# Gates of both token blocks of a recurrence unit computed together, recurrences one step later

## The chip, the cores and the metric

The kernel runs on one core of one Trainium2 chip. A core has five engines, each with its own in-order queue: TensorE (PE in the profile, with its weight loads shown as PEld), VectorE (DVE), ScalarE (ACT), GpSimd (POOL) and SyncE (SP, which issues the DMAs). The metric is the device time of one execution in microseconds; lower is better.

## The reference

One decoder layer on 2048 tokens of width 1024, in float32. Two token mixers work side by side on one input projection: four heads of a gated linear recurrence with a 128x128 state (HGRN2), and a gated real recurrence of width 512 behind a causal convolution (RG-LRU). Then come an output projection, a SwiGLU feed-forward of width 2816 and a final norm.

```python
xn = rms_norm(h, mix_norm_w)
q, f_logit, i_v, g, lru_x, lru_gate = split(xn @ w_in)
# HGRN2, per head, chunks of 32 tokens
f = lb + (1 - lb) * sigmoid(f_logit);  k = 1 - f;  b = cumsum(log(f))
scores = tril((silu(q) * exp(b)) @ (k * exp(-b)).T)
o = scores @ v + (silu(q) * exp(b)) @ state
state = exp(b_last) * state + (k * exp(b_last - b)).T @ v
# RG-LRU, width 512
xc = causal_conv4(lru_x) + conv_b
r = sigmoid(blockdiag(wa) @ xc + ba);  ig = sigmoid(blockdiag(wx) @ xc + bx)
a = exp(-8 * r * softplus(-a_param))
h_t = a * h_{t-1} + sqrt(1 - a*a) * (ig * xc)
y = h * gelu(lru_gate)
h = h + concat(rms(o) * silu(g), y) @ w_out
h = h + (silu(gate) * up) @ w_down;  out = rms_norm(h)
```

## The kernel before

The sequence is worked in two halves of 1024 tokens, each of two blocks of 512 (`c` = 0, 1). For each half the mixer runs first: values `v` (tiles `pv`), then eight steps `s` = 0 to 7, then the output gate (`pg`), the transposes `tp_o` and the output projection (`po` with a half number, `poh` in the profile). After both mixers come the feed-forward stages of both halves (`quad_*`, `pda`, `pdb`). Every 128x512 product is three matmuls per 128 rows of contraction (a high part times high and low part, and low times high), so a projection of one block (`feat_mm`, tiles `pa` and `pb`) is 24 matmuls.

Even steps work one HGRN2 head, odd steps one RG-LRU unit (128 of the 512 channels). A tile's name carries its step and its block: `lg_4_0` belongs to step 4, block 0. For each step and block the code computes `pa`, calls `run_pending`, computes `pb`, and then the first part of the step:

- HGRN2, `hg_pre`: ACT takes two sigmoids (`sq`, `sf`), a logarithm (`lg`, L257) and four exponentials (`eb` L262, `nx` L279 and L278, `lg` L280); DVE takes a running sum (`b`) and some fifteen products, the last of the line that PE needs being `lg` at L315. Its later parts wait in the list `pend`: `hg_mid` (PE transposes `lg` into `pk`, L329; products `pc`; DVE copies `pk` to `kut`; PE forms `pu` from it) and `hg_post` (PE forms `po`).
- RG-LRU, `lru_pre`: convolution on DVE, the GeLU branch `gl` on ACT, and a split of `xc` into `xh` and `xl`. Its later part is one function, `lru_post`: six matmuls into `pr` and `pi`, two sigmoids (`r`, `ig`), a tanh (`t`), an exponential (over `r`), DVE products, a square root (over `t`), a scan and the product `y`.

`run_pending` calls the next part of everything in `pend`, so `lru_post` of block 0 is written into block 1 of the same step, and that of block 1 into block 0 of the next step, which is an HGRN2 step.

[...]

The order in which the instructions of one engine stand is not the order of the code: a scheduler orders them when the program is built, by a model of its own, and on the chip every engine then takes its queue strictly in that order. The pools matter to it: tag `pg` has 16 pages of 128x512, tag `late` has 5, and PSUM has 4 banks under the tag `mm` (for `pa`, `pb`, `pg`) and 4 under `aux` (for `pr`, `pi`, `pk`, `pc`, `pu`, `po`, `tp_o`).

Of the kernel before, what the change touches and what calls it, by code (L numbers as in the profile page):

```python
# [35 lines left out]
def hybrid_layer(ctx: ExitStack, tc: tile.TileContext, x, x_t, norm_w, cols, w_in, gate_w, w_out, w_gu, w_down, out):  # L36
# [10 lines left out]
    def page(nm, dt=F32):  # L47
        return sb.tile([P, CW], dt, tag="pg", name=nm, bufs=16)
# [5 lines left out]
    def block(nm, dt=F32R):  # L54
        return sb.tile([P, 4, CW], dt, tag="bt", name=nm, bufs=14)
# [7 lines left out]
    def late(nm):  # L63
        return sb.tile([P, CW], F32, tag="late", name=nm, bufs=5)
# [4 lines left out]
    def aux(nm):  # L69
        return psp.tile([P, CW], F32, tag="aux", name=nm)  # L70
# [142 lines left out]
    def act_tile(nm):  # L213
        return [[block(f"{nm}_{s}{n}") for n in range(2)] for s in range(2)]

    def part(xt, s, k, ts=slice(0, CW)):
        return xt[s][k // 4][:, k % 4, ts]
# [7 lines left out]
    def transpose_in(dst, tt, n, src, nm, scale=None):  # L225
        split([dst[s][n][:, :, tt * P : (tt + 1) * P] for s in range(2)], transposed(tt, n, src, nm), scale)

    def feat_mm(w, xt, nm):
        ps = bank(nm)
        whi, wlo = w  # L230
        for k in range(KT):
            hi, lo = part(xt, 0, k), part(xt, 1, k)
            ks = slice(k * P, (k + 1) * P)
            nc.tensor.matmul(ps, lhsT=whi[:, ks], rhs=hi, start=(k == 0), stop=False)  # L234
            nc.tensor.matmul(ps, lhsT=wlo[:, ks], rhs=hi, start=False, stop=False)  # L235
            nc.tensor.matmul(ps, lhsT=whi[:, ks], rhs=lo, start=False, stop=(k == KT - 1))  # L236
        return ps

    def tok_mm(w4, xt, tt, nm):
        ps = bank(nm)  # L240
        tsl = slice(tt * P, (tt + 1) * P)
        for k in range(KT):
            whi, wlo = w4[k // 2]
            ks = slice((k % 2) * CW, (k % 2 + 1) * CW)
            hi, lo = part(xt, 0, k, tsl), part(xt, 1, k, tsl)
            nc.tensor.matmul(ps, lhsT=hi, rhs=whi[:, ks], start=(k == 0), stop=False)  # L246
            nc.tensor.matmul(ps, lhsT=hi, rhs=wlo[:, ks], start=False, stop=False)  # L247
            nc.tensor.matmul(ps, lhsT=lo, rhs=whi[:, ks], start=False, stop=(k == KT - 1))  # L248
        return ps
# [115 lines left out]
    def hg_post(h, st, vt, nm):  # L365
        hs = slice(h * P, (h + 1) * P)
        QI, S, sc = st["QI"], st["S"], st["sc"]
        po = aux("po" + nm)
        for n in range(TPC):
            ns = slice(n * P, (n + 1) * P)  # L370
            nc.tensor.matmul(po[:, ns], lhsT=QI[:, ns], rhs=S[n], start=True, stop=False)
            nc.tensor.matmul(po[:, ns], lhsT=sc[:, n, :], rhs=vt[:, n, hs], start=False, stop=True)
        ss = small.tile([P, TPC], F32, tag="oss", name="oss" + nm)
        jk = late("ojk" + nm)
        for n in range(TPC):
            ns = slice(n * P, (n + 1) * P)
            nc.scalar.activation(out=jk[:, ns], in_=po[:, ns], func=AF.Square, scale=float(P) ** -0.5, accum_out=ss[:, n : n + 1])
        v.tensor_scalar(out=ss, in0=ss, scalar1=EPS, scalar2=None, op0=ALU.add)
        nc.gpsimd.tensor_tensor(out=ss, in0=ss, in1=mhalf, op=ALU.pow)
        v.tensor_tensor(  # L380
            out=vt[:, :, hs], in0=po.rearrange("p (n e) -> p n e", e=P), in1=ss.unsqueeze(2).broadcast_to([P, TPC, P]), op=ALU.mult
        )


    def lru_pre(u, psx, psg, nm):
        xp = sb.tile([P, CW + 4], F32, tag="pg", name="xp" + nm, bufs=16)
        v.tensor_copy(out=xp[:, 0:3], in_=hist[:, u, :])
        nc.scalar.copy(out=xp[:, 3 : 3 + CW], in_=psx)
        nc.gpsimd.tensor_copy(out=hist[:, u, :], in_=xp[:, CW : CW + 3])
        gl = page("gl" + nm)  # L390
        nc.scalar.activation(out=gl, in_=psg, func=AF.Gelu_apprx_tanh)
        xc = page("xc" + nm)

        def cw(k):
            return par[:, C_CONVW + k * 4 + u : C_CONVW + k * 4 + u + 1]

        v.tensor_scalar(
            out=xc, in0=xp[:, 0:CW], scalar1=cw(0), scalar2=par[:, C_CONVB + u : C_CONVB + u + 1], op0=ALU.mult, op1=ALU.add
        )
        for k in range(1, 4):  # L400
            v.scalar_tensor_tensor(out=xc, in0=xp[:, k : k + CW], scalar=cw(k), in1=xc, op0=ALU.mult, op1=ALU.add)
        xh, xl = page("xh" + nm, dt=F32R), page("xl" + nm, dt=F32R)
        split((xh, xl), xc)
        return gl, xc, xh, xl


    def lru_post(u, gl, xc, xh, xl, y, nm):
        pr, pi = aux("pr" + nm), aux("pi" + nm)
        for m, pg in enumerate((pr, pi)):
            gs = slice((m * NU + u) * P, (m * NU + u + 1) * P)  # L410
            nc.tensor.matmul(pg, lhsT=gwh[:, gs], rhs=xh, start=True, stop=False)
            nc.tensor.matmul(pg, lhsT=gwl[:, gs], rhs=xh, start=False, stop=False)
            nc.tensor.matmul(pg, lhsT=gwh[:, gs], rhs=xl, start=False, stop=True)
        r, ig, t = late("r" + nm), late("ig" + nm), late("t" + nm)
        us = slice(u, u + 1)
        nc.scalar.activation(out=r, in_=pr, func=AF.Sigmoid, bias=par[:, C_BA + u : C_BA + u + 1])
        nc.scalar.activation(out=ig, in_=pi, func=AF.Sigmoid, bias=par[:, C_BX + u : C_BX + u + 1])

        nc.scalar.activation(out=t, in_=r, func=AF.Tanh, scale=msp[:, us])
        nc.scalar.activation(out=r, in_=r, func=AF.Exp, scale=nmsp[:, us])  # L420
        v.tensor_tensor(out=ig, in0=ig, in1=xc, op=ALU.mult)
        v.tensor_tensor(out=xc, in0=r, in1=r, op=ALU.mult)
        v.scalar_tensor_tensor(out=t, in0=xc, scalar=1.0, in1=t, op0=ALU.add, op1=ALU.mult)
        nc.scalar.activation(out=t, in_=t, func=AF.Sqrt)
        v.tensor_tensor(out=ig, in0=ig, in1=t, op=ALU.mult)
        v.tensor_tensor_scan(out=t, data0=r, data1=ig, initial=hst[:, us], op0=ALU.mult, op1=ALU.add)
        nc.gpsimd.tensor_copy(out=hst[:, us], in_=t[:, CW - 1 : CW])
        v.tensor_tensor(out=y[:, u, :], in0=t, in1=gl, op=ALU.mult)
# [505 lines left out]
    for half in range(2):  # L934
# [26 lines left out]
                    later.pop(0)()  # L961
        ys = [block(f"y{half}_{c}", F32) for c in range(NC)]

        pend = []

        def run_pending():
            for p in pend:
                p.pop(0)()
            pend[:] = [p for p in pend if p]

        for s in range(8):
            i = s // 2
            ws.ahead(2)
            wa, wb = ws.take(2)
            ws.ahead(2)
            for c in range(NC):
                nm = f"{half}_{s}_{c}"
                pa = feat_mm(wa, xt[c], "pa" + nm)
                run_pending()
                pb = feat_mm(wb, xt[c], "pb" + nm)  # L980
                if s % 2 == 0:
                    st = hg_pre(i, pa, pb, nm)
                    nxt = [
                        lambda i=i, st=st, c=c, nm=nm: hg_mid(i, c, st, vts[c], nm),
                        lambda i=i, st=st, c=c, nm=nm: hg_post(i, st, vts[c], nm),
                    ]
                else:
                    r = lru_pre(i, pa, pb, nm)
                    nxt = [lambda i=i, r=r, c=c, nm=nm: lru_post(i, *r, ys[c], nm)]
                pend.append(nxt)  # L990
        wg = ws.take(4)
        mixes = []
        for c in range(NC):
            for tt in range(TPC):
                ps = tok_mm(wg, xt[c], tt, f"pg{half}_{c}_{tt}")
                run_pending()
                sg = page(f"sg{half}_{c}_{tt}")
                nc.scalar.activation(out=sg, in_=ps, func=AF.Silu)
                v.tensor_tensor(out=vts[c][:, tt, :], in0=vts[c][:, tt, :], in1=sg, op=ALU.mult)
            mx = act_tile(f"mx{half}_{c}")  # L1000
            for tt in range(TPC):
                transpose_in(mx, tt, 0, vts[c][:, tt, :], f"o{half}_{c}_{tt}", par[:, C_HN : C_HN + 1])
            for u in range(NU):
                split([part(mx, s, 4 + u) for s in range(2)], ys[c][:, u, :])
            mixes.append(mx)
# [30 lines left out]
        for c in range(NC):  # L1036
            todo = len(steps[c])
            for n in range(2):
                wo = ws.take(4)
                for tt in range(TPC):  # L1040
                    g = c * TPC + tt
                    nm = f"h{half}_{g}_{n}"
# [14 lines left out]
                    i = n * TPC + tt + 1  # L1057
# [108 lines left out]
```

## Time and profile before

| | before |
|---|---|
| median of three runs | 2135.84 us (2135.84 to 2138.68) |
| profiled execution | 2136.71 us, span of its instructions 2135.0 us |
| TensorE busy | 2104.3 us, 99% of the span |
| VectorE busy | 1493.7 us, 70% |
| ScalarE busy | 1010.3 us, 47% |
| mean granted TensorE clock | 0.995 |
| first mixer, about 60 to 340 us; second, about 470 to 740 us | steps 0 to 7, then `pg` |

TensorE is busy nearly all the time, so what matters is where it isn't, and where its granted clock (1.00 is full speed) drops. The timeline gives each instruction's start and length in microseconds, and in brackets how long its engine was idle before it and who ended the wait. A matmul's length is longer than its distance to the next one, since matmuls overlap; distances between starts are what counts.

### The profile page before, as it was taken

Reading aid. Unit: us, or ns where it says so; the run is one execution under the profiler, and the core shown is the slowest. Engines: PE = TensorE matmul, PEld = TensorE weight load, DVE = VectorE, ACT = ScalarE, POOL = GpSimd, SP = SyncE. Lnnn points to the kernel's source line nnn. Section 1 sums busy time; section 2 is a strip of 40 time slices with the busy share of each in tenths; the row PEclk is TensorE's granted clock in tenths of the full one; section 3 lists DMA queues with packets and bytes.
Section 4 is the critical chain, followed back from the end, with each engine's and each line's share of the span. In section 5 each row is a group of like instructions: output and inputs, shape, how many; then the busy total and the mean of one; then the engine's idle time right before and its main releaser. Section 6 shows DMA issues by size and latency. Waiting matters only on the chain.

```text
span 2135.0 us, 26155 instructions
## 1 busy us (share of the span) xinstructions
PE 2104.3 (99%) x9704; PEld 1737.9 (81%) x9704; DVE 1493.7 (70%) x2415; ACT 1010.3 (47%) x1647; POOL 84.7 (4%) x130
## 2 busy tenths in 40 slices
PE   8999999999999999999999999999999999999998
PEld 6887888888877888788888888888788888888887
DVE  6577664645777566877667669878867667669787
ACT  5577764536777644533333334335333333334333
POOL 2000000100000000000000000000000000000000
PEclk9999999999999999999999999999999999999999
DMA  6111105851101058433223266345423223257424
GB/s 221 56 40 40 40 20 167 288 160 57 40 30 40 20 191 263 146 102 124 98 89 114 89 218 231 114 138 186 144 94 113 98 87 127 94 202 253 157 88 143
DMA packets 138420, 262.84 MB, mean 123 GB/s; under 512 B 11186, under 2 KB 27570, under 8 KB 138292
## 3 DMA queue, kind: packets, MB, share of 16 engines
q1 hardware_dynamic: 138292, 261.17, 36.6%
q8 instruction: 76, 1.25, 0.2%
q14 instruction: 52, 0.43, 0.1%
HBM read 197.95 MB, written 63.18 MB: 122 GB/s over the span
## 4 chain that ended last, share of the span: by engine, by line
PE 87%; ACT 6%; DVE 5%; DMA 1%; issue 1%; SPq 0%; POOL 0%; DVEq 0%; POOLq 0%; ACTq 0%
PE quad_e L614 11%; PE quad_g L614 11%; PE quad_a L614 11%; PE pda L882 10%; PE pdb L882 7%; PE quad_f L614 6%; PE poh L247 3%; PE poh L248 3%; PE poh L246 3%; PE pb L234 2%; PE pb L236 2%; PE pb L235 2%; PE pa L234 1%; PE pa L235 1%; PE pg L248 1%; PE pg L246 1%
## 5 line engine op out<-in xcount | busy, mean ns | idle before, releaser
L614 PE MATMUL quad_e<-act_e,wgu_e 128*128 128x512 f32 x528 | 129.6, 395 | 1.9 <-ACT wgu_e L207 1.9
L614 PE MATMUL quad_f<-act_f,wgu_f 128*128 128x512 f32 x528 | 127.9, 390 | 2.2 <-ACT wgu_f L207 1.5
L614 PE MATMUL quad_a<-act_a,wgu_a 128*128 128x512 f32 x528 | 127.5, 389 | 0.0
L614 PE MATMUL quad_g<-act_g,wgu_g 128*128 128x512 f32 x528 | 127.5, 390 | 0.0
L614 PE MATMUL quad_a<-act_b,wgu_b 128*128 128x512 f32 x528 | 127.3, 389 | 0.0
L614 PE MATMUL quad_g<-act_d,wgu_d 128*128 128x512 f32 x528 | 127.0, 389 | 0.1
L614 PE MATMUL quad_e<-act_c,wgu_c 128*128 128x512 f32 x528 | 126.9, 389 | 0.0
L614 PEld LDWEIGHTS quad_e<-act_e,wgu_e 128*128 128x128 f32 x528 | 100.4, 191 | 23.6 <-ACT wgu_e L207 2.4
L614 PEld LDWEIGHTS quad_f<-act_f,wgu_f 128*128 128x128 f32 x528 | 99.2, 188 | 23.9 <-ACT wgu_f L207 1.8
L498 DVE TENSOR_TENSOR u<-u,quad_g 128x512 f32<-128x512 f32 x88 | 60.5, 687 | 81.9 <-PE quad_g L614 81.9
L614 PEld LDWEIGHTS quad_g<-act_d,wgu_d 128*128 128x128 f32 x528 | 99.0, 188 | 21.0 <-DVE u L498 0.5
L614 PEld LDWEIGHTS quad_g<-act_g,wgu_g 128*128 128x128 f32 x528 | 99.1, 188 | 20.8 <-DVE wgu_g L208 0.3
L614 PEld LDWEIGHTS quad_a<-act_b,wgu_b 128*128 128x128 f32 x528 | 99.2, 188 | 20.6
L614 PEld LDWEIGHTS quad_e<-act_c,wgu_c 128*128 128x128 f32 x528 | 99.1, 188 | 20.6
L614 PEld LDWEIGHTS quad_a<-act_a,wgu_a 128*128 128x128 f32 x528 | 99.0, 188 | 20.5
L234 PE MATMUL pa<-xn,whi_in 128*128 128x512 f32 x256 | 102.0, 398 | 0.0
L234 PE MATMUL pb<-xn,whi_in 128*128 128x512 f32 x256 | 101.5, 397 | 0.0
L235 PE MATMUL pb<-xn,wlo_in 128*128 128x512 f32 x256 | 101.3, 396 | 0.0
L236 PE MATMUL pb<-xn,whi_in 128*128 128x512 f32 x256 | 101.2, 395 | 0.0
L235 PE MATMUL pa<-xn,wlo_in 128*128 128x512 f32 x256 | 100.8, 394 | 0.0
L236 PE MATMUL pa<-xn,whi_in 128*128 128x512 f32 x256 | 100.8, 394 | 0.0
L247 PE MATMUL poh<-wlo_o,mx 128*128 128x512 f32 x256 | 99.8, 393 | 0.6 <-DVE wlo_o L164 0.6
(331 smaller groups left out, 4944.6 us busy)
## 6 DMA issues: line engine op xcount, KB each, us to landing
raw<-in_w_gu SPq DMA_DIRECT2D x88, 512.0 KB, 3.8
raw_in<-in_w_in SPq DMA_DIRECT2D x48, 512.0 KB, 3.5
ao_p<-as SPq DMA_DIRECT2D x76, 256.0 KB, 2.6
raw_o<-in_w_out SPq DMA_DIRECT2D x32, 512.0 KB, 4.5
x<-in_x SPq DMA_DIRECT2D x32, 256.0 KB, 6.0
xrh<-in_x SPq DMA_DIRECT2D x32, 256.0 KB, 3.9
h<-h SPq DMA_DIRECT2D x32, 256.0 KB, 3.7
hn<-hths SPq DMA_DIRECT2D x32, 256.0 KB, 3.4
```

Of the source, the lines that this page charges most:

```text
L234: nc.tensor.matmul(ps, lhsT=whi[:, ks], rhs=hi, start=(k == 0), stop=False)
L235: nc.tensor.matmul(ps, lhsT=wlo[:, ks], rhs=hi, start=False, stop=False)
L236: nc.tensor.matmul(ps, lhsT=whi[:, ks], rhs=lo, start=False, stop=(k == KT - 1))
L246: nc.tensor.matmul(ps, lhsT=hi, rhs=whi[:, ks], start=(k == 0), stop=False)
L247: nc.tensor.matmul(ps, lhsT=hi, rhs=wlo[:, ks], start=False, stop=False)
L248: nc.tensor.matmul(ps, lhsT=lo, rhs=whi[:, ks], start=False, stop=(k == KT - 1))
L498: (e or v).tensor_tensor(out=out, in0=a, in1=b, op=op)
L614: nc.tensor.matmul(ps, lhsT=w[:, s, ks], rhs=x, start=first and k + n == 0, stop=k == 3 and n == 2, skip_group_check=not first)
L882: nc.tensor.matmul(ps, lhsT=x, rhs=y, start=first and q + n == 0, stop=q == gr.n - 1 and n == 2, skip_group_check=not first)
```

## The change

`lru_post` is cut into three: `lru_gates` (the six matmuls, both sigmoids, the tanh), `lru_exp` (the exponential) and `lru_end` (the rest). The gates of block 0 are held back by one place in `pend`, so that the gates of both blocks of a unit are written at the same place, in block 0 of the following step, behind its `pa`. The exponentials of both follow at the end of that block, and `lru_end` of both in its block 1 (after step 7: in the first tiles of `pg`). `r` and `ig` move from the pool of 5 to the pool of 16 pages. The arithmetic is the same.

```diff
-    def lru_post(u, gl, xc, xh, xl, y, nm):
+    def lru_gates(u, gl, xc, xh, xl, nm):
...
-        r, ig, t = late("r" + nm), late("ig" + nm), late("t" + nm)
+        r, ig, t = page("r" + nm), page("ig" + nm), late("t" + nm)
...
         nc.scalar.activation(out=t, in_=r, func=AF.Tanh, scale=msp[:, us])
+        return r, ig, t
+
+    def lru_exp(u, r, ig, t, xc):
+        us = slice(u, u + 1)
         nc.scalar.activation(out=r, in_=r, func=AF.Exp, scale=nmsp[:, us])
+
+    def lru_end(u, r, ig, t, gl, xc, y):
...
+        def gates(i, r, c, nm):
+            gated.append((i, c, lru_gates(i, *r, nm), r[0], r[1]))
+
+        def run_exp():
+            for i, c, (r, ig, t), gl, xc in gated:
+                lru_exp(i, r, ig, t, xc)
+            done = gated[:]
+            gated.clear()
+            if done:
+                pend.append([lambda: [lru_end(i, r, ig, t, gl, xc, ys[c]) for i, c, (r, ig, t), gl, xc in done]])
...
-                    nxt = [lambda i=i, r=r, c=c, nm=nm: lru_post(i, *r, ys[c], nm)]
+                    nxt = [lambda i=i, r=r, c=c, nm=nm: gates(i, r, c, nm)]
+                    if c == 0:
+                        nxt.insert(0, lambda: None)
                 pend.append(nxt)
+                run_exp()
...
                 run_pending()
+                run_exp()
```

What the scheduler made of it differs from the written order, and it is the same in both halves. The built program has 119 table loads on ACT instead of 115. Three places show what moved.

The first place is ACT's queue between the gates of step 3 and the logarithm of step 4. Before, it begins behind all of `r_3_0` (which stands ahead of `xh_3_1`):

```order
L424 ACTIVATE t_3_0_1553<-t_3_0_1553 128x512
L416 ACT_TABLE_LOAD
L416 ACTIVATE r_3_1_1651<-pr_3_1_1643,par 128x512
L417 ACTIVATE ig_3_1_1652<-pi_3_1_1644,par 128x512
L419 ACTIVATE t_3_1_1653<-r_3_1_1651,tinies 128x512
L420 ACT_TABLE_LOAD
L420 ACTIVATE r_3_1_1651<-r_3_1_1651,tinies 128x512
L255 ACT_TABLE_LOAD
L255 ACTIVATE sf_4_0_1692<-pb_4_0_1666 128x512
L257 ACT_TABLE_LOAD
L257 ACTIVATE lg_4_0_1693<-sf_4_0_1692,tinies 128x512
```

Now, on the same engine, from the exponential of block 0 on (its sigmoids and tanh stand just ahead):

```order
L425 ACTIVATE r_3_0_1628<-r_3_0_1628,tinies 128x512
L417 ACT_TABLE_LOAD
L417 ACTIVATE r_3_1_1642<-pr_3_1_1634,par 128x512
L420 ACTIVATE t_3_1_1644<-r_3_1_1642,tinies 128x512
L432 ACT_TABLE_LOAD
L432 ACTIVATE t_3_0_1630<-t_3_0_1630 128x512
L418 ACT_TABLE_LOAD
L418 ACTIVATE ig_3_1_1643<-pi_3_1_1635,par 128x512
L254 ACTIVATE sq_4_0_1673<-pa_4_0_1595 128x512
L425 ACT_TABLE_LOAD
L425 ACTIVATE r_3_1_1642<-r_3_1_1642,tinies 128x512
L255 ACT_TABLE_LOAD
```

The work of both blocks now stands between `xh_3_1` and the logarithm of step 4, and block 0's exponential is still taken ahead of block 1's sigmoid, with a load on each side.

The second place is PE's queue around the transposes `pk_4_0`, the first thing that PE needs of head step 4's chain. Before:

```order
L236 MATMUL pa_5_0_1866<-xn_0_11_165,whi_in_14_1608 128x512
L329 MATMUL pk_4_0_1756<-ident,lg_4_0_1693 128x128 x4
L337 MATMUL pc_4_0_1763<-W_4_0_1716,nx_4_0_1702 64x128
L337 MATMUL pc_4_0_1763<-eb_4_0_1701,nx_4_0_1702 64x64
L234 MATMUL pa_5_0_1866<-xn_0_01_163,whi_in_14_1608 128x512
```

Now:

```order
L236 MATMUL pb_5_0_1942<-xn_0_10_164,whi_in_15_1591 128x512
L329 MATMUL pk_4_0_1740<-ident,lg_4_0_1675 128x128 x4
L337 MATMUL pc_4_0_1747<-W_4_0_1698,nx_4_0_1684 64x128
L337 MATMUL pc_4_0_1747<-eb_4_0_1683,nx_4_0_1684 64x64
L234 MATMUL pb_5_0_1942<-xn_0_00_162,whi_in_15_1591 128x512
```

Before, `pk_4_0` stood behind 21 of the 24 matmuls of `pa_5_0`; now it stands behind all 24 and 6 of `pb_5_0`, 9 matmuls later. In the same way `pk_2_0` moves from 8 to 7 matmuls of `pb_3_0`, and `pk_6_0` from 18 of `pa_7_0` to 24 and 7 of `pb_7_0`. The gates of both blocks of a unit stand behind `pa` of the next step (in step 4, `pr_3_0` right behind the last matmul of `pa_4_0`) and in its `pb`; after step 7 they stand behind `pg` tile 0 and in tile 1.

The third place is ACT's queue in the `pg` tiles behind step 7. Before:

```order
L998 ACTIVATE sg_0_1_2658<-pg_0_1_2633 128x512
L416 ACT_TABLE_LOAD
L416 ACTIVATE r_7_1_2615<-pr_7_1_2607,par 128x512
L417 ACTIVATE ig_7_1_2616<-pi_7_1_2608,par 128x512
L419 ACTIVATE t_7_1_2617<-r_7_1_2615,tinies 128x512
L420 ACT_TABLE_LOAD
L420 ACTIVATE r_7_1_2615<-r_7_1_2615,tinies 128x512
L424 ACT_TABLE_LOAD
L424 ACTIVATE t_7_1_2617<-t_7_1_2617 128x512
L998 ACT_TABLE_LOAD
L998 ACTIVATE sg_0_2_2686<-pg_0_2_2661 128x512
```

Now:

```order
L418 ACTIVATE ig_7_1_2607<-pi_7_1_2599,par 128x512
L1021 ACT_TABLE_LOAD
L1021 ACTIVATE sg_0_0_2614<-pg_0_0_2559 128x512
L425 ACT_TABLE_LOAD
L425 ACTIVATE r_7_1_2606<-r_7_1_2606,tinies 128x512
L1021 ACT_TABLE_LOAD
L1021 ACTIVATE sg_0_1_2658<-pg_0_1_2617 128x512
L432 ACT_TABLE_LOAD
L432 ACTIVATE t_7_1_2608<-t_7_1_2608 128x512
L1021 ACT_TABLE_LOAD
L1021 ACTIVATE sg_0_2_2686<-pg_0_2_2661 128x512
```

`sg` is the SiLU of an output gate tile; DVE multiplies it into `v` (L999, now L1022), and PE transposes that into `tp_o`. Before, only block 1's part of unit 7 stood ahead of `sg_0_2`; now both blocks' parts do, and the SiLUs stand between exponential and square root. The queues of SP and POOL, and so the DMA issues, stand in the same order as before.

More of the change, by code (lines that the diff above doesn't have):

```diff
@@ L419, in lru_post @@
         nc.scalar.activation(out=t, in_=r, func=AF.Tanh, scale=msp[:, us])
+        return r, ig, t
+    def lru_exp(u, r, ig, t, xc):
+        us = slice(u, u + 1)
         nc.scalar.activation(out=r, in_=r, func=AF.Exp, scale=nmsp[:, us])
+    def lru_end(u, r, ig, t, gl, xc, y):
+        us = slice(u, u + 1)
         v.tensor_tensor(out=ig, in0=ig, in1=xc, op=ALU.mult)
@@ L962, in hybrid_layer @@
         ys = [block(f"y{half}_{c}", F32) for c in range(NC)]
-        pend = []
+        pend, gated = [], []
+        def gates(i, r, c, nm):
[7 more added lines that the diff above has]
+                pend.append([lambda: [lru_end(i, r, ig, t, gl, xc, ys[c]) for i, c, (r, ig, t), gl, xc in done]])
         def run_pending():
```

## The prediction

> **What bounds the kernel now.** I read the page's busy shares first, then TensorE's list of waits, then its windows around the waits, then ACT's and DVE's timeline in them.
>
> ```profile
> span 2135.0 us, 26155 instructions
> PE 2104.3 (99%) x9704; PEld 1737.9 (81%) x9704; DVE 1493.7 (70%) x2415; ACT 1010.3 (47%) x1647; POOL 84.7 (4%) x130
> ...
> PE pk L329 <- DVE lg L315: 6.4, 3, 2.9
> ...
> PE pu L354 <- DVE kut L331: 3.8, 2, 1.9
> ```
>
> PE is idle for 30.7 us of 2135.0 in all. No matmul is added or removed, so the change can act only through these idle times, through new ones, and through PE's clock. In the mixers the waits are those of `pk` for the end of the head's chain on DVE (`lg`, L315), and of `pu` for the copy behind it. The windows (columns: length, PE busy, clock, then DMA) show where, two per half:
>
> ```profile
> 200.00:212.00 12.00, 9.13 (x50) 0.86 0.28 89
> 264.00:273.00 9.00, 6.46 (x35) 1.00 0.00 1
> 612.00:628.00 16.00, 13.09 (x64) 0.89 0.20 67
> 680.00:692.00 12.00, 10.12 (x47) 0.86 0.09 32
> ```
>
> PE is idle in them for 2.87, 2.54, 2.91 and 1.88 us, 10.2 in all: head step 4 and head step 6 of each half. In three of them the clock fell too: 12 x 0.14, 16 x 0.11 and 12 x 0.14 us are each about 1.7 us of PE time lost on top. In the second it stayed at 1.00. So a wait of some 3 us costs about 4.6. [...]
>
> **The mechanism.** Before `pk`, ACT must finish the head's chain, and the RG-LRU work of the step before stands in ACT's queue among it. ACT's timeline gives each step's price as the distance to the next start:
>
> ```profile
> 174.73 0.69 ACT L416 ACTIVATE r<-pr,par 128x512 f32<-128x512 f32 x1
> 175.32 0.68 ACT L417 ACTIVATE ig<-pi,par 128x512 f32<-128x512 f32 x1
> 175.88 0.72 ACT L419 ACTIVATE t<-r,tinies 128x512 f32<-128x512 f32 x1
> ...
> 178.43 0.72 ACT L420 ACTIVATE r<-r,tinies 128x512 f32<-128x512 f32 x1
> 179.18 1.28 ACT L254 ACT_TABLE_LOAD   x1
> 180.47 0.60 ACT L254 ACTIVATE sq<-pa 128x512 f32<-128x512 f32 x1
> ...
> 182.38 0.63 ACT L424 ACTIVATE t<-t 128x512 f32<-128x512 f32 x1
> ...
> 191.46 0.82 ACT L257 ACTIVATE lg<-sf,tinies 128x512 f32<-128x512 f32 x1
> ...
> 195.53 0.63 ACT L262 ACTIVATE eb<-b 128x512 f32<-128x512 f32 x1
> ...
> 196.38 0.40 ACT L278 ACTIVATE nx<-lg 128x256 f32<-128x256 f32 x1
> 196.81 0.63 ACT L280 ACTIVATE lg<-lg 128x512 f32<-128x512 f32 x1
> 197.46 1.28 ACT L254 ACT_TABLE_LOAD   x1
> ...
> 199.25 1.04 ACT L163 CAST whi_in<-raw_in 128x1024 fp32r<-128x1024 f32 x1
> ...
> 266.00 0.63 ACT L262 ACTIVATE eb<-b 128x512 f32<-128x512 f32 x1 [0.45 <-DVE b L259]
> ```
>
> So: `r` 0.59, `ig` 0.56, `t` 0.74, exponential of `r` 0.75, a load 1.29, `sq` (also `sf`, `sg`) 0.61, square root 0.65, `lg` 0.83, `eb` with the first `nx` 0.85, second `nx` 0.43, last exponential 0.65, cast 1.05, and 0.45 for `b` where no other work covers it.
>
> ```profile
> L424 ACT ACT_TABLE_LOAD x16 | 20.5, 1283 | 0.3
> ```
>
> Sixteen loads have 0.3 us of idling ahead of them in all, and the activation behind one starts with its end (179.18 + 1.28 to 180.47). [...]
>
> DVE's steps behind it (a step is 0.08 shorter than its length, as 198.75 to 199.89 shows):
>
> ```profile
> 195.46 1.28 DVE L426 TENSOR_TENSOR_SCAN t<-r,hst,ig 128x512 f32<-128x512 f32 x1
> ...
> 198.75 1.22 DVE L164 TENSOR_TENSOR wlo_in<-raw_in,whi_in 128x1024 fp32r<-128x1024 f32 x1
> 199.89 0.42 DVE L314 TENSOR_TENSOR lg<-sf,lg 128x256 f32<-128x256 f32 x1
> ...
> 200.63 0.68 DVE L256 TENSOR_TENSOR sq<-sq,pa 128x512 f32<-128x512 f32 x1
> ...
> 201.50 0.29 DVE L318 TENSOR_TENSOR lg<-lg,G 128x128 f32<-128x128 f32 x1
> ...
> 202.45 0.42 DVE L315 TENSOR_TENSOR lg<-nx,G 128x256 f32<-128x256 f32 x1
> ```
>
> **When PE starts the chains, and when it needs them.** In the changed order the gates of block 0 stand right behind `pa` of the head step, so the new chain starts when `pr` ends. At these rows of before, PE has done the same work as after the new `pi` (the last: `pg`, plus its 24 matmuls):
>
> ```profile
> 121.05 0.39 PE L234 MATMUL pb<-xn,whi_in 128*128 128x512 f32 x1
> ...
> 177.47 0.39 PE L234 MATMUL pb<-xn,whi_in 128*128 128x512 f32 x1
> ...
> 237.71 0.39 PE L234 MATMUL pb<-xn,whi_in 128*128 128x512 f32 x1
> 243.15 0.39 PE L234 MATMUL pa<-xn,whi_in 128*128 128x512 f32 x1
> ...
> 290.48 0.39 PE L246 MATMUL pg<-whi_in,xn 128*128 128x512 f32 x1
> ```
>
> 24 matmuls take 5.44 us (237.71 to 243.15), 0.227 each. The last matmul of `pr` starts four steps before these rows and lasts 0.39: `pr` is there at 120.54 (step 2), 176.96 (step 4), 237.20 (step 6) and 290.48 + 5.44 - 0.51 = 295.41 (`pg`). PE reaches the places that wait at:
>
> ```profile
> 146.04 0.60 PE L329 MATMUL pk<-ident,lg 128*128 128x128 f32 x4
> ...
> 199.76 0.39 PE L236 MATMUL pa<-xn,whi_in 128*128 128x512 f32 x1
> 203.02 0.63 PE L329 MATMUL pk<-ident,lg 128*128 128x128 f32 x4 [2.87 <-DVE lg L315]
> ...
> 259.53 0.60 PE L329 MATMUL pk<-ident,lg 128*128 128x128 f32 x4
> ...
> 313.66 1.47 PE L222 MATMUL tp_o<-ident,v 128*128 128x128 f32 x12
> ```
>
> With the new places of `pk` (1 matmul earlier, 9 and 13 later): 145.8, 200.15 + 2.04 = 202.2, 259.53 + 2.95 = 262.5; the third group of `tp_o`, 8 of 12 transposes in, at 314.5. Times are in the frame of before; a wait at one place moves all that is behind it alike.
>
> **The change part by part.** Splitting the function, the list `gated` and the pages cost no instruction. Six matmuls per block move behind the next `pa`: PE does the same work. The four extra loads are 5 us of ACT, inside the chains. SP and POOL keep their order, so no DMA moves. With `r` and `ig` in pages, 8 RG-LRU pages and 8 of a head fill the 16; I find no wait in the queues that this adds on another engine, and bound it by 0 and the longest new wait. Odd steps lose block 0's gates on ACT and DVE; nobody on PE waits there, so that gains nothing. What counts are four chains per half:
>
> - Step 2. ACT: `r`, `ig`, `t`, exponential, square root, then `r`, `ig`, `sq`, `t`, `sf`, exponential, `lg`, 0.45 for `b`, `eb` and `nx`, square root, `nx`, last exponential: 11.0 us, and 8 loads, 10.3. From 120.54 that ends at 141.9. Then a load and `sq` of block 1 (1.9), for which DVE stands: `sq` 0.60, scan 1.20, two half-size steps 0.68, a tiny one 0.07, a quarter 0.20, `y` 0.60, `wlo` 1.14, L315 0.42, together 4.9. `pk` can go at 148.7 against 145.8: 2.9 us, where before has none.
> - Step 4. The first load waits for `pr`. 17 ACT steps with the cast, 11.6, and 10 loads, 12.9: from 176.96 to 201.5; load and `sq` 1.9; DVE 3.4 (no scan, no `y`). 206.8 against 202.2: 4.6.
> - Step 6. The same without the cast, with `b`: 11.0 and 11 loads 14.2: 237.20 to 262.4; 1.9; DVE 4.9. 269.2 against 262.5: 6.7. The later wait for `kut` goes, since its copy then has 22 matmuls of time.
> - `pg`. To the end of block 1's square root 7.8 of steps and 9 loads, 11.6: 295.41 to 314.8; DVE product 0.61, scan 1.20, `y` 0.60, product with `sg` 0.69, and the `tp_o` group can go at about 318.0 against 314.5: 3.5, where before has none.
>
> That is 17.7 us per half, 35.4 in all, against 10.2: plus 25.2. Each of the eight waits is as long as those that let the clock fall, against three before. Five falls at 1.7 are 8.5. A fall's price lies between 0 (the window at 264) and, behind a longer wait, an estimated twice 1.7; I take 1.7, the value of three of four windows. Sum 33.7. The profiled execution took 2136.7, 0.9 above the median of the runs: 2170.4, so I say 2170.
>
> **Rivals.**
> - Faster. The later place of `pk` decides: if the new chain in step 4 ended no later than the old one (L315 near 202.9), the wait there would be 0.7 instead of 2.9 and the clock would hold: 3.9 us less per half, with the waits of step 6 gone too (2.5 and 1.9 + 1.7), 13.9 in all: 2123. Against it: ACT would have to be done near 197.5 in step 4, 4 us before the row sum, and ACT has no gap to give. 3 in 100.
> - No change beyond 0.2% (about what a measurement of this kernel can tell from none, 4.3 us): the waits only move, 2136. It needs chains about 3 us shorter throughout. 4 in 100.
> - Half of it: the chains are 1.5 us shorter at each place and steps 2 and `pg` keep their clock: 12 and 6.8 less, about 2151. 8 in 100 for 2141 to 2151.
> - More: the five new falls twice as dear, and each of the eight chains 1 us longer from waits for pages: 8.5 + 8 more, 2187 and up. 5 in 100.
> - A load holds ACT for twice its row: 82 x 1.28 = 105 more, about 2275. The rows speak against it. 1 in 100.
>
> **How the numbers follow.** The forecast holds 79 in 100 between 2151 and 2187: its ends are 1.5 us off each chain with two falls less, and the dearer falls with 1 us on each. Faster by over 0.2% 0.03, within 0.04, slower 0.93.
>
> **What would show it.** Right: PE's waits for `lg` L315 at six places, about 14 us per half, the longest in step 6; two waits of `tp_o`, 3 to 4 us; the clock under 0.9 around most; ACT with 119 loads. Wrong: `tp_o` and step 2 without waits (the chain's price is too high), or a clock of 1.00 behind them. What I may have missed is a wait inside ACT's chain for DVE or a page, which would make every term longer.

## The result, and the profile after

The changed kernel takes 2176.1 us (median of 4 runs, 2175.3 to 2177.4), against 2137.3 us for the kernel before in the same session: a ratio of 1.0179 (95% interval 1.0167 to 1.0191), 38.8 us more. The forecast was 2170 with a range of 2151 to 2187.

The busy shares of the changed kernel, to be held against those of before:

```profile
span 2174.0 us, 26170 instructions
PE 2114.8 (97%) x9704; PEld 1746.3 (80%) x9704; DVE 1495.9 (69%) x2415; ACT 1016.6 (47%) x1651; POOL 83.7 (4%) x130
```

The span grew by 39.0 us. PE's matmuls are as many as before, and so the whole difference splits in two: PE is idle for 2174.0 - 2114.8 = 59.2 us instead of 30.7 (28.5 more), and busy for 2114.8 instead of 2104.3 (10.5 more, for the same work: mostly a lower clock, as the windows further down show). PE's list of waits (total, times, longest) says where the idle time is:

```profile
PE pk L329 <- DVE lg L315: 30.6, 6, 7.1
PE tp_o L222 <- DVE v L1022: 8.1, 2, 4.0
```

These eight waits make 38.7 us. Before, the waits of the mixers made 11.1: 6.4 of `pk`, 3.8 of `pu` for `kut` and 0.9 of `po` for `sct`. The last two are gone. Four of the eight rows of PE's timeline, those of the first half, with the idle time in brackets:

```profile
150.03 0.63 PE L329 MATMUL pk<-ident,lg 128*128 128x128 f32 x4 [3.09 <-DVE lg L315]
211.97 1.08 PE L329 MATMUL pk<-ident,lg 128*128 128x128 f32 x4 [5.17 <-DVE lg L315]
276.65 1.08 PE L329 MATMUL pk<-ident,lg 128*128 128x128 f32 x4 [7.10 <-DVE lg L315]
331.96 0.78 PE L222 MATMUL tp_o<-ident,v 128*128 128x128 f32 x4 [4.05 <-DVE v L1022]
```

The four of the second half wait 3.09, 5.12, 7.04 and 4.00 us. The four places are the same in both halves: head steps 2, 4 and 6, and the third group of `tp_o`.

ACT's timeline shows the chain behind the wait of step 4, from the first load, which waits for `pr`, to the last exponential of the head:

```profile
181.62 1.28 ACT L417 ACT_TABLE_LOAD   x1 [2.22 <-PE pr L414]
182.91 0.69 ACT L417 ACTIVATE r<-pr,par 128x512 f32<-128x512 f32 x1
...
186.84 1.28 ACT L417 ACT_TABLE_LOAD   x1
...
194.04 1.28 ACT L425 ACT_TABLE_LOAD   x1
...
196.07 1.28 ACT L255 ACT_TABLE_LOAD   x1
...
205.44 0.63 ACT L280 ACTIVATE lg<-lg 128x512 f32<-128x512 f32 x1
```

ACT does not idle in it. It runs for 24.45 us (181.62 to 206.07), of which ten loads are 12.9. Sigmoid, exponential and square root alternate between the two blocks, and each alternation is a load.

That alone does not set it apart from the kernel before, where only the sigmoids and the tanh of block 0 stood ahead of `xh_3_1` (176.50); its exponential and square root stood behind it. From the load ahead of block 0's `r` to the head's last exponential (173.44 to 197.44, 24.0 us) there were ten loads as well:

```profile
173.44 1.28 ACT L416 ACT_TABLE_LOAD   x1
```

What differs in step 4 is the start. PE does the same work at 177.47 before and at 182.07 now, 4.60 us later, so the old start would be at 178.04. ACT begins at 181.62, because it now has to wait for `pr_3_0`, which PE forms behind `pa_4_0`. In steps 2 and 6 the loads grow too: from `xh` of block 1 (L207) to the head's last exponential (L280) ACT's timeline has 3, 9 and 4 loads in steps 2, 4 and 6 before, and 9, 10 and 11 now (first half).

### The profile page after: what moved, and what is told of

Its sections match the earlier page's. It is cut to its first block, busy times and chain, and to the rows that moved or that the text cites. A ratio compares the mean times of both kernels' runs of the same rounds, so it can differ in the third digit from the quotient of the medians.

```text
span 2174.0 us, 26170 instructions
## 1 busy us (share of the span) xinstructions
PE 2114.8 (97%) x9704; PEld 1746.3 (80%) x9704; DVE 1495.9 (69%) x2415; ACT 1016.6 (47%) x1651; POOL 83.7 (4%) x130
## 4 chain that ended last, share of the span: by engine, by line
PE 86%; ACT 7%; DVE 4%; issue 1%; DMA 1%; POOL 0%; SPq 0%; DVEq 0%; POOLq 0%; ACTq 0%
PE quad_e L622 11%; PE quad_g L622 11%; PE quad_a L622 11%; PE pda L890 10%; PE pdb L890 7%; PE quad_f L622 5%; PE poh L246 3%; PE poh L247 3%; PE poh L248 3%; PE pb L235 2%; PE pa L235 2%; PE pa L234 2%; PE pa L236 2%; PE pb L234 2%; PE pb L236 2%; PE pv L246 1%
## 5 line engine op out<-in xcount | busy, mean ns | idle before, releaser
L622 PEld LDWEIGHTS quad_f<-act_f,wgu_f 128*128 128x128 f32 x528 | 99.3, 188 | 25.2 <-ACT act_g L207 2.2
L248 PE MATMUL poh<-whi_o,mx 128*128 128x512 f32 x256 | 99.9, 391 | 0.0
```

The source lines that it names most:

```text
L622: nc.tensor.matmul(ps, lhsT=w[:, s, ks], rhs=x, start=first and k + n == 0, stop=k == 3 and n == 2, skip_group_check=not first)
```

## The experiments

The theory: block 0's gates, exponential and square root now stand in ACT's queue among the head's activations, interleaved with block 1's, and the table loads of that order make `lg` late. The rivals: the pool of pages holds the head's tiles back, the split functions with the held-back recurrence make DVE late, or the loads only stand in time that passes anyway.

**Which part of the change.** Four kernels, in one session (before: 2137.5 us).

`e1`: the changed kernel without

```
-                    if c == 0:
-                        nxt.insert(0, lambda: None)
```

> The changed kernel, but the gates of block 0 stay one place earlier (the empty first entry is taken out), so the two blocks' gates are not together; the split functions, the held-back recurrence and the pages stay. Theory (block 0's ACT work inside the head's chain makes the waits): in the head steps only block 1's work stands in the chain, 5 to 6 loads in place of 10 in step 4, so step 2 and the third tp_o group do not wait, steps 4 and 6 wait 2 to 3 us as before: 2137, between 2131 and 2145. Rival (the held-back recurrence or the pages make them): 2155 to 2180.

Measured 2134.8 us, ratio 0.9987 (0.9977 to 0.9996). The split, the held-back recurrence and the pages together cost nothing. The time came out as expected, the places did not: `pk` waits six times, 4.5 us in all, in head steps 4 and 6, and `po` waits three times for `sct`, 5.0 in all, of which 1.92 and 1.91 are the first in each half, of head step 2.

`e2`: the kernel before with those two lines put in behind `nxt = [lambda ...: lru_post(...)]`.

> The kernel before, but block 0's whole post-processing one place later, so that both blocks' gates stand behind the same pa; no split, no held-back recurrence, old buffers. Theory: the chain in step 4 has 9 loads in place of the changed kernel's 10, the waits are there but about 1.3 us shorter: PE waits in steps 2, 4 and 6 of 1.5 to 6 us each, 2168, between 2155 and 2178. Rival (split or pages make the waits): 2137.

Measured 2171.2 us, ratio 1.0152 (1.0137 to 1.0168). Its waits:

```profile
PE pk L329 <- DVE lg L315: 23.3, 6, 5.9
PE tp_o L222 <- DVE v L1001: 10.8, 2, 5.4
```

The two lines alone bring 33.7 of the 38.8 us. The waits of `pk` are 7.3 us shorter in all, 1.2 each, about as forecast, those of `tp_o` 1.4 longer each. Its program has 113 loads, two fewer than the kernel before, and nine of them in step 4 between `xh` and the head's last exponential, as many as before. So the number of loads alone does not make the wait.

`e3`: the changed kernel with

```
-        r, ig, t = page("r" + nm), page("ig" + nm), late("t" + nm)
+        r, ig, t = late("r" + nm), late("ig" + nm), late("t" + nm)
```

> The changed kernel with r and ig back in their old pool. Theory: the pages are not the cause; 9 or 10 loads still stand in each chain: 2174, between 2166 and 2181, with six waits of pk. Rival (the pages' pool holds the head's tiles back): 2140 to 2155.

Measured 2174.3 us, ratio 1.0171 (1.0153 to 1.0188).

`e4`: the kernel before with the opposite edit.

> The kernel before with r and ig in the pool of pages, nothing else. Theory: 5 loads in the chain of step 4 as before, 2138, between 2131 and 2146. Rival (the pool makes the waits): 2155 to 2175.

Measured 2135.8 us, ratio 0.9987 (0.9977 to 0.9997). With `e3` this clears the pages in both directions: they bring neither the eight waits nor any time. They do change the order: `pk` waits 4.5 us and `po` for `sct` 6.1, where before has 6.4 and 0.9, and 3.8 of `pu`.

**Is it the loads?** `e5` and `e6` are the changed kernel and the one before with

```
-        nc.scalar.activation(out=r, in_=r, func=AF.Exp, scale=nmsp[:, us])
+        nc.scalar.activation(out=r, in_=r, func=AF.Tanh, scale=nmsp[:, us])
...
-        nc.scalar.activation(out=t, in_=t, func=AF.Sqrt)
+        nc.scalar.activation(out=t, in_=t, func=AF.Tanh)
```

> The changed kernel with the RG-LRU's exponential and square root both replaced by Tanh (another function computed, so another output): as many ACT instructions, but 61 table loads in place of 119, in the chain of step 4 about 3 in place of 10. Theory (what the chains cost is mostly their table loads): 7 loads of 1.28 us less are 9 us, more than every wait, so all eight waits go and the clock holds: 2122, between 2115 and 2132. Rival (the order of the activations and DVE's queue make the waits, the loads only stand in time that would pass anyway): waits of 2 us or more stay at six places or more, 2145 to 2176.

> The kernel before with the same replacement, as the control: 77 loads in place of 115, 3 or so fewer in the chains of steps 4 and 6. Theory: the four waits of 10.2 us in all and three falls of the clock at 1.7 go: 2121, between 2115 and 2129, the same as the changed kernel with Tanh within 5 us. Rival: 2130 to 2138.

Measured, against before at 2137.3 us in that session: 2118.8 us for the changed kernel (ratio 0.9918, 0.9903 to 0.9934) and 2119.1 us for the one before (0.9916, 0.9902 to 0.9929). In the trace of `e5` the instructions of ACT and DVE stand in the order of the changed kernel, one by one; with 58 of its 119 loads gone, all 39 us of the difference are gone, and the old waits with them. So the later start costs nothing where the chain is this much shorter: the wait needs both, the start behind `pa` and the loads. Two windows over the mixers of the changed kernel with Tanh (length, PE busy, clock) show PE with no idle time in either half; in the same windows of the changed kernel PE is busy for 220.59 and 220.75 us, at a clock of 0.96 and 0.95:

```profile
100.00:340.00 240.00, 240.00 (x1247) 1.00 0.13 42
540.00:780.00 240.00, 240.00 (x1225) 1.00 0.21 66
```

With no wait in the mixers the program takes about 2119 us: that is an estimate of the floor for reordering them.

**Moving the work out of the chain.** `e7`: the kernel before, block 1's `lru_post` one place later. `e8`: the changed kernel, both blocks' gates one place later still.

```
e7 +                    if c == 1:
e7 +                        nxt.insert(0, lambda: None)
e8 -                    if c == 0:
e8 -                        nxt.insert(0, lambda: None)
e8 +                    nxt[:0] = [lambda: None] * (2 - c)
```

> The kernel before with block 1's whole post-processing one place later (block 0's stays), so that nothing of the RG-LRU stands in the chain of the head's block 0; it stands in that of block 1. Theory: the waits of pk for block 0 go; block 1's pk waits as little as in the kernel before, where none shows, since block 1's chain starts without a cast and with PE later: 2123, between 2117 and 2133. Rival (the same distance, the same wait, only at block 1's pk): 2137, up to 2150 if the third tp_o group waits too.

> The changed kernel with both blocks' gates one place later still, behind pa of block 1's head. 99 loads in place of 119; no RG-LRU work stands in block 0's chain, 7 loads and both blocks' work stand in block 1's. Theory: no waits for block 0; for block 1 waits 3 loads (3.9 us) shorter than the changed kernel's 3.1, 5.1 and 7.1, so 0 to 3 us, and a third tp_o group that waits some 3 us: 2143, between 2128 and 2160. Rival (PE is not yet at block 1's pk by then, nothing waits): 2122.

`e7` measured 2134.9 us (0.9986, 0.9977 to 0.9995; same session), and the rival was right: the wait only moved to block 1's `pk`. PE's timeline, first half:

```profile
155.78 0.30 PE L329 MATMUL pk<-ident,lg 128*128 128x128 f32 x1 [0.58 <-DVE lg L315]
213.70 0.30 PE L329 MATMUL pk<-ident,lg 128*128 128x128 f32 x1 [1.88 <-DVE lg L315]
271.58 0.30 PE L329 MATMUL pk<-ident,lg 128*128 128x128 f32 x1 [1.85 <-DVE lg L315]
```

`e8` measured 2159.2 us (1.0104, 1.0090 to 1.0117), inside its range, but by neither mechanism that was written down. No `pk` waits at all, and `tp_o` for only 3.5 us in two waits; PE's list names another one:

```profile
PE po L372 <- DVE sct L349: 21.0, 6, 3.5
```

The place one slot later is where ACT and DVE, in turn, bring block 0's scores (`sct`) out of PSUM for `po`. ACT's timeline in step 4 shows the three copies of one such group among loads of the RG-LRU and the head:

```profile
211.08 0.45 ACT L351 COPY sct<-pc 32x384 f32<-32x384 f32 x1
211.55 1.28 ACT L262 ACT_TABLE_LOAD   x1
...
213.89 0.36 ACT L351 COPY sct<-pc 32x256 f32<-32x256 f32 x1
...
217.50 0.26 ACT L351 COPY sct<-pc 32x128 f32<-32x128 f32 x1
```

The copies themselves take 1.1 us, but from the first to the end of the third 6.7 us pass. DVE's copies stand between other work in the same way; which of the two queues holds the last one back was not separated.

**Ordering it instead.** In `e9` both exponentials of the changed kernel are ordered on ACT behind the last exponential of the head (an edge that sets the order and costs no instruction). `e10` does the same in the `pg` stage, behind the third SiLU. `e11` is `e1` with block 1's exponential ordered like this.

```
e9, e10, e11 (hg_pre):
-        nc.scalar.activation(out=lg, in_=lg, func=AF.Exp)
+        last[0] = nc.scalar.activation(out=lg, in_=lg, func=AF.Exp)
e9, e10 (run_exp; e11 for block 1 alone):
-                lru_exp(i, r, ig, t, xc)
+                with tc.issue_after(last[0].ins):
+                    lru_exp(i, r, ig, t, xc)
e10 (the pg loop):
-                run_exp()
                 sg = page(f"sg{half}_{c}_{tt}")
-                nc.scalar.activation(out=sg, in_=ps, func=AF.Silu)
+                last[0] = nc.scalar.activation(out=sg, in_=ps, func=AF.Silu)
                 v.tensor_tensor(out=vts[c][:, tt, :], in0=vts[c][:, tt, :], in1=sg, op=ALU.mult)
+                if tt == TPC - 2:
+                    run_exp()
```

> The changed kernel with both exponentials of the RG-LRU ordered on ACT behind the last exponential of the head of block 0; nothing else. 87 loads in place of 119, in the chains of steps 2, 4 and 6 three (Sigmoid, Ln, Exp) in place of 8 to 11. The pg stage keeps its order nearly. Theory (loads and order are the cause, and the gates together are harmless): the six waits of pk go, the two of tp_o (4.0 each with a fall of the clock of some 2) stay: 2119 with nothing left, plus 12, makes 2131, between 2122 and 2142. Rival (the two square roots and the block 1 chain now make po wait for its sct copies, as in the kernel with the gates one place later): 2145 to 2165.

> The same, and in the pg stage the exponentials of step 7 stand behind the third Silu: 79 loads. Theory: the waits of tp_o go too: 2120, between 2115 and 2130, below the kernel before by 0.4 to 1.0%. Rival (po waits for sct, or tp_o for the recurrence now ahead of the last product): 2133 to 2160.

> The kernel with block 0's gates at their own place, and block 1's exponential ordered behind the last exponential of the head of block 0: 105 loads. Theory: the waits of pk of 0.5 to 1.8 us go, 3 loads fewer stand in their chain; those of po for sct (5.0 in all) stay: 2127, between 2119 and 2133. Rival (no gain, the waits only move to po): 2135.

Measured, against before at 2138.1 us in that session: `e9` 2130.1 us (0.9961, 0.9948 to 0.9973), `e10` 2121.8 us (0.9926, 0.9912 to 0.9939), `e11` 2122.6 us (0.9930, 0.9918 to 0.9943). All three lie inside the theory's ranges. `e11` is below its middle since the waits of `po` for `sct` went too, which the theory had staying. ACT's timeline of `e9` in step 4:

```profile
176.07 1.28 ACT L419 ACT_TABLE_LOAD   x1 [2.69 <-PE pr L416]
...
184.23 1.28 ACT L259 ACT_TABLE_LOAD   x1
...
186.36 1.28 ACT L264 ACT_TABLE_LOAD   x1
...
189.37 0.63 ACT L282 ACTIVATE lg<-lg 128x512 f32<-128x512 f32 x1
189.91 1.32 ACT L427 ACTIVATE r<-r,tinies 128x512 f32<-128x512 f32 x2
```

The same gates of both blocks, computed together, have one load here for Sigmoid, Tanh and the head's Sigmoids (176.07), one for the logarithm (184.23) and one for all exponentials (186.36): three instead of ten. The chain is 13.9 us long (176.07 to 190.0) instead of 24.45, although it now waits 1.97 us for PE's `pb` in the middle. Seven loads are 9.0 us of that; the exponentials and square roots of both blocks, some 2.8 us, now also stand behind the chain. In the mixers `e9` keeps two waits of `tp_o` of 2.5 us each (4.0 were expected), in the `pg` stage that its edit does not order; `e10` removes them. `e10` and `e11` both beat the kernel before by 0.7%, and their intervals overlap: with the order on ACT put right, no difference between gates together and apart shows. The two differ in the order of the `pg` stage as well, so this is no clean comparison.

## Why the prediction was right

**The direction and the mechanism** were right: the chain on ACT ahead of `pk` became longer than PE's matmuls that cover it, at the four places named. `e2` and `e5` show the two halves of the argument, that it is block 0's place and that the chain is too long because of its loads.

**The start of the chains.** Forecast for step 4: 176.96 in the frame of before. PE is 4.60 us later there (177.47 and 182.07 for the same work), which gives 181.56; the first load of step 4 starts at 181.62. Of the 4.60 us, 0.93 stood ahead of step 2 already (121.05 and 121.98), so step 2 cost 3.67 more than before, not the 3.09 + 1.7 of its wait and fall. The forecast had before lose nothing in step 2, and that was wrong: from `pb` of step 2 to `pb` of step 4 PE took 56.4 us before (121.05 to 177.47), 60.1 in the changed kernel and 55.2 in `e5` (121.92 to 177.11), which has no wait in the mixers. The 4.9 us of the changed kernel over `e5` are the wait and the fall. Before had lost 1.2 us there: 0.47 in a wait of `po` for `sct` at 155.59, and some 0.8 where pairs of `po`'s matmuls begin 0.92 and 0.78 us apart (157.55, 158.47, 159.25) instead of 0.44 (170.65, 171.09).

**The chains on ACT.** Step 2: 21.6 us from `r` (121.48 to 143.05) against 21.3. Step 4: 24.45 against 24.5. Step 6: 25.5 (244.17 to 269.67) against 25.2. The price of a load, 1.28 us, held: in step 4 the next activation starts 1.29 us after its load does (181.62 to 182.91). Nothing of the last rival appears, in which each of 82 loads (9, 11, 12 and 9 in the four chains of a half) costs twice that.

**The waits.** 2.9, 4.6, 6.7 and 3.5 us were forecast per half, 17.7; 3.09, 5.17, 7.10 and 4.05 were measured in the first half, 19.4, and 38.7 in both against 35.4. Each place is 0.2 to 0.6 us longer. In step 4 DVE is late: it has no idle time there and comes to block 1's `sq` at 208.45, 0.47 after ACT has finished it (207.98); from there to `pk` at 211.97 it is 3.5 us, against 3.4. The forecast had DVE stand and wait for `sq`. In step 6 it does stand; there the chain on ACT is 0.3 longer and the tail 0.2 (271.59 to 276.65, 5.06 instead of 4.9). In `pg` the chain, from its first load to the end of block 1's square root, is 19.8 instead of 19.4 (308.69 to 328.46), and the tail 3.5 to `tp_o` at 331.96 instead of 3.1 to 3.2. The removed wait of `pu` did go, as said.

**The clock.** This is the term that was mis-sized: 8.5 us for five new falls at 1.7 each. At five of the eight places the low clock lasts twice as long, which I had put only into the rival "more". The windows below are cut so that the clock changes at their edges (length, PE busy, clock); first two around step 2, then three around step 4 and four around step 6, and two behind the wait of step 2 in the second half:

```profile
148.04:151.45 3.41, 1.42 (x20) 1.00 0.17 31
151.45:154.86 3.41, 3.41 (x11) 0.50 0.32 125
206.06:209.48 3.42, 0.74 (x4) 1.00 0.48 144
209.48:212.89 3.41, 0.92 (x4) 0.50 0.23 50
212.89:216.30 3.41, 3.41 (x20) 0.50 0.29 118
267.50:270.92 3.42, 2.05 (x10) 1.00 0.13 28
270.92:274.33 3.41, 0.00 (x0) 1.00 0.33 126
274.33:277.74 3.41, 1.09 (x6) 0.50 0.15 31
277.74:281.16 3.42, 3.42 (x20) 0.50 0.37 129
584.94:588.35 3.41, 2.79 (x20) 0.50 0.48 154
588.35:591.77 3.42, 3.42 (x9) 0.50 0.01 2
```

In step 2 PE works for 3.41 us at half clock and loses 1.7. In step 4 it works for 0.92 + 3.41 us at half clock and loses up to 2.2; in step 6 1.09 + 3.42, up to 2.3. The waits of 5.17 and 7.10 us thus cost about half a microsecond more in clock than that of 3.09, not a second 1.7, since PE worked in only 0.92 and 1.09 us of the first of their two low stretches. But the length of the wait does not decide it. Step 2 of the second half waits 3.09 us as well; there the wait reaches 0.62 us into the next window, the clock stays low for another one, and PE loses up to (2.79 + 3.42) / 2 = 3.1 us.

Worked out like this for all eight places, the falls cost up to 17.2 us, against 5.1 for the three of before: 12.1 more, where 8.5 were forecast.

**The sum.** From the first matmul of `pa` to the first of `poh`, both halves together, PE took 554.0 us before, 591.0 in the changed kernel and 534.9 in `e5`. The changed kernel's 56.1 over `e5` are its waits and falls (38.7 + 17.2). Of the 19.1 of before, waits and falls are 16.2 (11.1 + 5.1); the other 2.9 stand in no wait of the list. Some 0.8 of them are the slow pairs of `po` above, the rest was not located. They are gone in the changed kernel, and the forecast did not have them. So the mixers grew by 37.0 us: 27.6 in waits and 12.1 in falls, less some 2.9. The other 2.0 of the 39.0 passed outside the mixers, where the change does nothing; single runs of before lie 4 us apart. The forecast of 33.7 was low in the waits and the falls, and part of that was offset by these 2.9 us, of which it did not know: that part of its closeness is luck.

The lower end of the range, 2151, goes by four falls less, as in the rival "half of it"; with two less in all it would be 2155.

## What to carry to other kernels

Computing two blocks together saves table loads only if their activations stand together in the queue of the engine that runs them: here the code grouped the gates and the scheduler's order took them apart, so the change brought four loads more, and an order-only edge in the same place took 32 away. The number of loads in the whole program is a poor sign, though: `e2` has two fewer than the kernel before and is 33.7 us slower. What counts is what stands between the operand that starts the chain and the engine that waits at its end, and when that operand comes. Before moving work to another place in the program, ask what stands in the queue there and who is waited for behind it: one place later the wait passed from `pk` to `po` (`e8`) or from block 0 to block 1 (`e7`), and only shortening the chain removed it. A wait of the busiest engine came with a price in its clock here: some 3 us idle cost 1.7 us more, and up to 3.1 in one place.

## What the runs showed of the hardware

In the traces of the changed kernel and of the one before, the clock falls on a grid. In the mixers of the changed kernel the eight low stretches begin at 151.45, 209.48, 274.33, 332.36, 584.94, 646.38, 711.24 and 769.26 us. From the first to the last are 617.81 us, 181 steps of 3.4133, and the six between lie on the same steps within 0.01 us. Each stretch lasts 3.41 or 6.83 us. In the kernel before the three falls of the mixers (204.43, 620.86, 685.71) are 122 and 19 such steps apart.

Some falls came behind less than a whole step of idling. In step 2 above, 1.99 of the 3.41 us were idle and the clock fell, 1.4 us after PE had begun to work again. The windows of the kernel before show a fall behind 1.88 us and none behind 1.48, and those of `e7` (the last four rows) that the idle time alone does not part the two:

```profile
265.87:269.28 3.41, 1.93 (x14) 1.00 0.00 0
269.28:272.70 3.42, 2.76 (x15) 1.00 0.00 0
682.30:685.71 3.41, 1.53 (x11) 1.00 0.00 0
685.71:689.12 3.41, 3.41 (x11) 0.50 0.00 0
268.23:271.65 3.42, 1.57 (x8) 1.00 0.00 0
271.65:275.06 3.41, 3.41 (x34) 1.00 0.00 0
626.63:630.04 3.41, 1.67 (x12) 1.00 0.00 0
630.04:633.45 3.41, 3.41 (x25) 0.50 0.00 0
```

The first and the third row hold the wait of `pu` for `kut`, 1.88 us each time. In the first half the grid cuts it, 1.48 us fall into one window and the clock holds; in the second all 1.88 us fall into one and the clock drops. In `e7` a window with 1.85 us idle was followed by full clock and one with 1.74 by a fall. Over the windows on the grid of the changed kernel and the one before, from 20 us on, none at full clock with up to 1.48 us idle was followed by a fall, and all fifteen with 1.88 or more were; what decides in `e7` these runs do not show. Of the windows at low clock in the two, the thirteen without idle time were followed by full clock, and the seven with 0.62 to 2.49 us idle by another low one. That settles the window at 264 of the prediction, where a wait of 2.54 us cost no clock: those were two waits, 1.88 and 0.66 us, in different windows. Whether a wait of some 2 us cost 1.7 us more was thus partly a matter of where the grid lay in that run.

In the programs of this case Tanh stands behind Sigmoid without a load between them (`t` at 175.88 behind `ig` in the prediction's rows), and behind Exp as well: in `e8` an Exp at 200.21 and a Tanh at 200.84 follow one load (198.92), so the exponential of one block and the Tanh of the other share it there. Exp straight behind Ln has one (`e9`: a load for Ln at 184.23, the next for Exp at 186.36).
